# One group of a two-level Strassen-Winograd kernel makes its product S3 x T3 plainly, and the sums of T3's quarters come behind it

## The chip, the core and the metric

The kernel runs on one core of a Trainium2 chip. The time is in device microseconds, from three runs of the same program; the median is given. One further execution was recorded by the profiler, and all times of single instructions come from it. The engines are called PE (TensorE, the matmuls), PEld (its weight loads), DVE (VectorE), ACT (ScalarE), POOL (GpSimd) and SP (SyncE, whose queue issues nearly all DMAs). Each engine works through its own queue in order.

## The reference

```python
def reference(x, w):                       # x: 8 x 2048 x 2048, w: 2048 x 2048, f32
    cs = np.cumsum(x, axis=1)
    diff = cs - np.concatenate([zeros, cs[:, :-1, :]], axis=1)
    return np.matmul(diff, w).astype(np.float32)
```

The difference of a running sum is the input again, so the kernel computes x times w: 16384 rows of x against a 2048 x 2048 matrix.

## The kernel before

The rows of x are cut into 128 row tiles of 128 rows. The first four are multiplied in a head stage while the weights are loaded, and w is scaled and kept on chip as f16 blocks. The rest is done in groups of four row tiles, named g, h (upper half of the two-by-two scheme) and k, l (lower half; k belongs to g, l to h). A group is one step of Winograd's form of Strassen's method: seven products P1 to P7 of half-size blocks, with sums S1 to S4 of x blocks and T1 to T4 of weight blocks. P7 is S3 x T3. The tiles 4 to 7 (`group_plain`) and 8 to 11 (`group_half`) are special; from tile 12 on 29 objects of the class `Group` follow, numbered 0 to 28 here. "The first group of the table" is group 0, tiles 12 to 15.

In a `Group`, P1, P2, P3, P4, P5 and P7 are made once more by seven: each is split into seven quarter products, written P7.p1 to P7.p7, of four 128x512 matmuls each (`quarter`, recorded at L592). Only P6 is made plainly (`whole`), as four pieces for tile g and four for tile h, P6g.0 to P6h.3, of four matmuls each (`steps`, recorded at L573). A product by seven costs 28 matmuls, a plain one 32. By seven it also needs sums on other engines:

- small sums of x quarters, P7.s1 to P7.s4 (128x512 f16, L561 on POOL or L563 on DVE);
- sums of weight quarters. Those that are wanted in every group are kept; the others are made anew in each group, as fills of the one buffer `flow` (P7.fp4, P7.fp5, P7.fp7; 128x2048 f16 on DVE, L958). The kept ones are made once, in or before group 0, by `less` (L555). For T3 they are two, `sums_of_T3` in the code: the first overwrites the quarter t12 of T3 itself with t12 - t11, the second makes t22 minus that. T3 can be used plainly only until the first of them;
- copies of finished quarters from their PSUM bank (ACT, P7.c1, c5, c6, c7 at L1086) and additions of them onto the banks that hold P1 + P6 (DVE, P7.a1, a5g, a5h, a6, a7h, a7k at L1061; P5.m1 and P5.m2 of product P5 have the same line).

The four banks g0, g1, h0, h1 hold P1 + P6 + P7 in the end. From them add.C22g0 to add.C22h1 take an output block (DVE, L603, scaled) and keep.C21... and P4 go on. The additions without a scale, such as add.C12g1.e, are L1127. Banks, buffers c of outputs and four scratch quarters are taken from lists, first freed first used.

What stands in which order is set by a table, `ORDER`: about 260 step names, each with the group it belongs to relative to the running one (P1.p1+1 is the next group's). The loop at the end of the function walks the table once per group and issues each step on its engine. So group 0's P7 is mixed with the end of its P5, with P3, with P4, and with the loading, scaling (weigh, scale, recip, narrow) and transposing (turn) of group 1's tiles. A dictionary `before` hangs the one-time sums of weights ahead of named steps of group 0. S1.g, S3.g, S3.h are the sums S of one tile (128x1024, L563).

Of the kernel before, what the change touches and what calls it, by code (L numbers as in the profile page):

```python
# [10 lines left out]
def kernel(  # L11
# [30 lines left out]
    PLAIN = 4  # L42
    KQ = KO // 4
    END = M // P
# [12 lines left out]
    B11, T1, B12, T2, B21, T3, B22, T4 = (  # L57
        [p[:, i // 2, i % 2] for p in pieces] for i in range(8)
    )
# [4 lines left out]
    def quarter_of(i, a, n):  # L64
        return blocks[:, i // 2, i % 2, ds(4 * a, 4), n, :]

    def spare_of(i, k):
        return blocks[:, i // 2, i % 2, ds(k, 2), :, :]
# [17 lines left out]
    def after(engine, ask):  # L86
        if engine in last:
            with tc.issue_after(last[engine].ins):
                said = ask()
        else:  # L90
            said = ask()
        last[engine] = said[-1] if isinstance(said, tuple) else said
        return said
# [100 lines left out]
    with ExitStack() as head:  # L194
        ring = [alone([P, NH], bf16, f"wb{i}", head) for i in range(7)]
        results = [alone([P, NB], f32, f"o{i}", head) for i in range(5)]
        first = head.enter_context(tc.tile_pool(name="first", bufs=1))
# [276 lines left out]
    class Part:  # L474
        def __init__(self, ap):
            self.all = ap
# [31 lines left out]
    class Inner:  # L508
# [7 lines left out]
        def first(self):  # L516
            less(self.Q1, self.t12, self.t11)
            less(self.Q2, self.t22, self.Q1)
# [19 lines left out]
    def in_twos(t):  # L538
        return t if len(t.shape) == 4 else t.rearrange("p (a b) n -> p a b n", b=2)
# [5 lines left out]
    def half_of(t, i):  # L545
        return in_twos(t)[:, i]
# [5 lines left out]
    def less(dst, p, q):  # L552
        if len(dst.shape) == 4 or len(p.shape) == 4 or len(q.shape) == 4:
            dst, p, q = in_twos(dst), in_twos(p), in_twos(q)
        after("dve", lambda: nc.vector.tensor_tensor(dst, p, q, SUB))  # L555
# [88 lines left out]
    in_5 = Inner(1, spare_of(2, 6), quarter_of(6, 1, 0), flow)  # L644
    in_1 = Inner(0, spare_of(2, 6), S1_all, flow)
# [316 lines left out]
    in_7 = Inner(5, None, quarter_of(5, 0, 1), None)  # L962
# [23 lines left out]
    LATE = 'C12g0 C12g1 C12h1 C12h0 C11g1 C11h1 C21g1 C21h1'.split()  # L986

    class Group:
        def __init__(self, g):
            self.late = LATE if g + 4 < END else ()  # L990
            self.tiles = dict(g=g, h=g + 2, k=g + 1, l=g + 3)
            self.at = {}
            self.do = {}
            self.sums = {}
            self.plan()
# [144 lines left out]
        def plan(self):  # L1140
            tiles = self.tiles
            half = {}
# [13 lines left out]
            def A(c, i):  # L1156
                return [half[c][i].half(n) for n in range(2)]

            x, z = ["h0", "h1", "g0", "g1"], ["zh0", "zh1", "zg0", "zg1"]
# [60 lines left out]
            self.add("C12h1", q, "q")  # L1220
            self.add("C12h0", q, "q", let=True)

            self.small_sums("P7", A("g", 0), A("h", 0), True)
            self.onto("P7", *x)
            for n, c in zip(x, ("C22h0", "C22h1", "C22g0", "C22g1")):
                self.add(c, n, "x")

# [73 lines left out]
    END_ORDER = """  # L1301
# [7 lines left out]
    group_plain(PLAIN, *pairs)  # L1309
    group_half(PLAIN + 4, *pairs[:2], *banks[4:])  # L1310
    open_banks += [banks[i] for i in (6, 7, 0, 1, 3, 5, 2, 4)]
    groups = [Group(g) for g in range(PLAIN + 8, END, 4)]
    for c in groups[0].tiles:
        for s in ("load", "weigh0", "weigh1", "scale", "recip", "unit", "narrow0", "narrow1", "turn0", "turn1"):
            del groups[0].do[f"{s}.{c}"]
# [3 lines left out]
    def first(*names):  # L1319
        return min(names, key=place_of.get)  # L1320

    def sums_of_T3():
        less(in_7.t12, in_7.t12, in_7.t11)
        less(in_7.Q2, in_7.t22, in_7.t12)

    before = {first("P5.s1", "P5.p5"): lambda: less(in_5.Q1, in_5.t22, in_5.Q2), first("P7.fp5", "P7.fp7", "P7.p6", "P7.fp4"): sums_of_T3, first("P1.s4", "P1.fp4", "P1.p6"): lambda: less(*(half_of(t, 0) for t in (in_1.Q2, in_1.t22, in_1.Q1))), first("P5.s3", "P5.p7"): in_5.third}
    for b in range(-early, len(groups) - late):
        for name, ahead in ORDER:
            i = b + ahead
            if 0 <= i < len(groups) and name in groups[i].do:  # L1330
                if i == len(groups) - 1 and name in END_ORDER:
                    continue
                if i == 0 and name in before:
                    before[name]()
                groups[i].do.pop(name)()
    for name in END_ORDER:
        groups[-1].do.pop(name)()
    assert not any(g.do for g in groups)
# [30 lines left out]
```

## Time and profile before

| what | us |
|---|---|
| median of three runs | 1464.87 (1464.37 to 1465.89) |
| the profiled execution, its own time | 1463.69 |
| its span, first to last instruction | 1461.9 |
| PE busy, 6563 matmuls | 1428.8 (98%) |
| DVE busy | 1408.8 (96%) |
| ACT busy | 1160.6 (79%) |
| POOL busy | 356.6 (24%) |

The profiled execution is 1.18 us shorter than the median. Of its time, 1.8 us lie outside the span. The granted clock of TensorE, in parts of the full one, is 0.996 over the whole span. Times of rows are counted from the span's start. In a timeline, instructions of one form that follow each other are one row: start, length, engine, line, operation, output <- inputs, how many, and in brackets the idle time of the engine before it with what ended that.

### The profile page before, as it was taken

The numbers are of one execution on the slowest core, as the hardware profiler recorded it, in microseconds if no ns is written. First come the engines' busy times: TensorE is split into PE (matmuls) and PEld (weight loads), VectorE is DVE, ScalarE is ACT, GpSimd is POOL, SyncE is SP. The second block draws the span as 40 slices with busy tenths as digits, with TensorE's granted clock in tenths as the row PEclk, the third lists the DMA queues.
The fourth block names the chain that finished last, engine by engine and source line by source line (L and its number), as shares of the span: only waits on it lengthen the run. The fifth ranks groups of instructions, "written<-read, shape, count | busy, mean of one in ns | idle before, by whom it ended". The sixth has DMA issues, their size and how long they took to land. (4 is left out here: it accounts for less than half of the span.)

```text
span 1461.9 us, 21138 instructions
## 1 busy us (share of the span) xinstructions
PE 1428.8 (98%) x6563; PEld 635.8 (43%) x6563; DVE 1408.8 (96%) x2367; ACT 1160.6 (79%) x1786; POOL 356.6 (24%) x422
## 2 busy tenths in 40 slices
PE   8999989999999999999999999999999999999997
PEld 3444434444444444444444444444444444444443
DVE  7998899999999999999999999999999999999998
ACT  5887558888788888887888888887888887788882
POOL 0111021223231223321223321222321223221221
PEclk9999999999999999999999999999999999999999
DMA  9999839999898989889998899998889999889992
GB/s 358 368 237 298 213 121 237 240 232 252 228 244 232 250 228 251 236 237 239 238 238 247 238 230 251 251 228 240 241 239 239 252 229 243 229 245 245 248 243 105
DMA packets 377761, 351.65 MB, mean 241 GB/s; under 512 B 274800, under 2 KB 274800, under 8 KB 377520
## 3 DMA queue, kind: packets, MB, share of 16 engines
q1 hardware_dynamic: 377088, 348.47, 88.0%
q0 software_dynamic: 560, 1.84, 0.3%
q8 instruction: 51, 0.84, 0.2%
q14 instruction: 62, 0.51, 0.1%
HBM read 150.99 MB, written 134.22 MB: 195 GB/s over the span
## 5 line engine op out<-in xcount | busy, mean ns | idle before, releaser
L592 PE MATMUL b<-W,x 128*128 128x512 f16 x2124 | 522.3, 380 | 8.2 <-DVE x L563 6.1
L592 PEld LDWEIGHTS <-x 128*128 128x128 f16 x2952 | 286.5, 98 | 372.3 <-DVE x L563 19.6
L1127 DVE TENSOR_TENSOR c<-b,c 128x512 f32<-128x512 f32 x504 | 332.6, 678 | 0.6 <-issue 0.3
L172 ACT ACTIVATE F<-F,of 128x1024 f16<-128x1024 f32 x246 | 283.0, 1150 | 32.6 <-DVE of L156 30.8
L125 ACT ACTIVATE waste<-F 128x1024 uint8<-128x1024 f32 x246 | 259.9, 1057 | 54.5 <-DMA F<-in_x_dram 51.8
L592 PEld LDWEIGHTS <-inner 128*128 128x128 f16 x1996 | 192.6, 98 | 250.3 <-DVE inner L563 27.2
L592 PE MATMUL b<-W,inner 128*128 128x512 f16 x1176 | 288.9, 380 | 1.1 <-DVE inner L563 0.5
L573 PE MATMUL b<-W,x 128*128 128x512 f16 x1216 | 278.0, 379 | 0.3 <-DVE x L563 0.2
L563 DVE TENSOR_TENSOR x<-x,x 128x1024 f16<-128x1024 f16 (+1 forms) x359 | 211.9, 597 | 9.6 <-DMA x<-F 6.3
L603 DVE SCALAR_TENSOR_TENSOR c<-b,of,c 128x512 f32<-128x512 f32 x286 | 209.6, 740 | 8.9 <-PE b L592 5.5
L592 PE MATMUL b<-flow,x 128*128 128x512 f16 x820 | 210.4, 379 | 5.3 <-DVE flow L958 4.3
L600 ACT ACTIVATE c<-b,of 128x512 f32<-128x512 f32 x268 | 178.1, 681 | 37.9 <-PE b L592 13.7
L142 POOL TENSOR_SCALAR of<-of 128x1 f32<-128x1 f32 x112 | 79.5, 710 | 470.1 <-ACT waste L125 412.5
L1061 DVE TENSOR_TENSOR b<-b,c 128x512 f32<-128x512 f32 x290 | 191.6, 687 | 0.2 <-PE b L592 0.2
L1116 ACT COPY c<-b 128x512 f32<-128x512 f32 x224 | 128.5, 579 | 71.4 <-DVE c L603 45.0
L958 DVE TENSOR_TENSOR flow<-W 128x2048 f16<-128x2048 f16 x145 | 184.2, 1270 | 0.0
L573 PEld LDWEIGHTS <-x 128*128 128x128 f16 x1216 | 118.6, 98 | 144.7 <-DVE x L563 7.1
L600 ACT ACTIVATE c<-c,of 128x512 f32<-128x512 f32 x224 | 154.8, 714 | 12.9 <-DVE c L1127 12.9
L592 PE MATMUL b<-inner 128*128 128x512 f16 x472 | 121.1, 379 | 0.0
L561 POOL TENSOR_TENSOR inner<-x 128x512 f16<-128x512 f16 x29 | 35.7, 1232 | 268.2 <-PE b L592 268.2
L561 POOL TENSOR_TENSOR x<-x,x 128x512 f16<-128x512 f16 x58 | 88.3, 1522 | 22.3 <-PE b L592 22.3
L1086 ACT COPY c<-b 128x512 f32<-128x512 f32 x116 | 68.2, 588 | 26.8 <-PE b L592 17.9
(78 smaller groups left out, 988.9 us busy)
## 6 DMA issues: line engine op xcount, KB each, us to landing
F<-in_x_dram SPq DMA_DIRECT2D x246, 512.0 KB, 5.8
out_dram<-c SPq DMA_DIRECT2D x492, 256.0 KB, 3.2
W<-in_w_dram SPq DMA_DIRECT2D x32, 512.0 KB, 9.7
W<-in_x_dram SPq DMA_DIRECT2D x16, 256.0 KB, 7.1
x<-F SPq DMA_TRANSPOSE x246, 3.5
out_dram<-o POOLq DMA_DIRECT2D x5, 256.0 KB, 3.9
out_dram<-o SPq DMA_DIRECT2D x5, 256.0 KB, 3.5
xP<-in_x_dram SPq DMA_DIRECT2D x1, 1024.0 KB, 5.3
```

The costliest lines, as they stand in the source:

```text
L125: lambda: nc.scalar.activation(waste, where[t][i], ABS, scale=1.0 / ROW, accum_out=sums_of[t][:, i : i + 1],),
L172: lambda: nc.scalar.activation(narrowed(t)[:, ds(i * NH, NH)], where[t][i], COPY, scale=s),
L561: after("pool", lambda: nc.gpsimd.tensor_tensor(dst.all, p.all, q.all, op))
L563: after("dve", lambda: nc.vector.tensor_tensor(dst.all, p.all, q.all, op))
L573: said = nc.tensor.matmul(to[n], a[k], b[k][:, n, :], start=(first and k == 0), stop=(k == KH - 1), skip_group_check=True,)
L592: said = nc.tensor.matmul(to, a[k], b[k], start=(first and k == 0), stop=(k == 3), skip_group_check=True)
L600: after("act", lambda: nc.scalar.activation(c, p, COPY, scale=u))
L603: after("dve", lambda: nc.vector.scalar_tensor_tensor(c, p, u, c, MUL, ADD))
L958: after("dve", lambda: nc.vector.tensor_tensor(in_twos(flow), x, y, op))
L1061: after("dve", lambda: nc.vector.tensor_tensor(t, p, s, ADD))
L1116: after("act", lambda: nc.scalar.copy(to, p))
L1127: after("dve", lambda: nc.vector.tensor_tensor(to, p, to, ADD))
```

## The change

In group 0 alone, P7 is made as a whole product like P6. Its sums, fills, copies and additions are not issued there. The pieces of the plain product take the places of some of the quarters in the table: P7g.0 stands where P7.p1 stood, P7g.1 to P7g.3 where P7.p5, P7.p6 and P7.p2 stood, P7h.0 and P7h.1 in the place of P7.a7k, P7h.2 and P7h.3 in that of P7.fp4. The two sums of T3 move from ahead of P7.fp5 to two later places of group 0: one ahead of add.C12g1.e, one ahead of add.C21h1.e. Groups 1 to 28 make P7 by seven, as before.

```diff
     class Group:
-        def __init__(self, g):
+        def __init__(self, g, more):
+            self.more = more
...
-            self.small_sums("P7", A("g", 0), A("h", 0), True)
-            self.onto("P7", *x)
+            if self.more:
+                self.small_sums("P7", A("g", 0), A("h", 0), True)
+                self.onto("P7", *x)
+            else:
+                self.whole("P7", T3, half["g"][0], half["h"][0], *x)
...
-    groups = [Group(g) for g in range(PLAIN + 8, END, 4)]
+    groups = [Group(g, g > PLAIN + 8) for g in range(PLAIN + 8, END, 4)]
...
-    def sums_of_T3():
-        less(in_7.t12, in_7.t12, in_7.t11)
-        less(in_7.Q2, in_7.t22, in_7.t12)
+    PLAINLY = {
+        "P7.p1": ["P7g.0"],
...
+        "P7.a7k": ["P7h.0", "P7h.1"],
+        "P7.fp4": ["P7h.2", "P7h.3"],
+    }
...
-    before = {..., first("P7.fp5", "P7.fp7", "P7.p6", "P7.fp4"): sums_of_T3, ...}
+    before = {..., "add.C12g1.e": lambda: less(in_7.t12, in_7.t12, in_7.t11), "add.C21h1.e": lambda: less(in_7.Q2, in_7.t22, in_7.t12), ...}
+    def go_on(i, name):
+        if i == len(groups) - 1 and name in END_ORDER:
+            return
+        if i == 0 and name in before:
+            before[name]()
+        for some in [name] if groups[i].more else PLAINLY.get(name, [name]):
+            if some in groups[i].do:
+                groups[i].do.pop(some)()
```

The instructions in their order, engine by engine. On DVE, group 0, from the sum that stands ahead of P5.s3 (`W<-W`, then P5.s3) on; before, T3's two sums follow (`x2`), then the fill P7.fp5, S3.h, a reciprocal, and P7.s1, whose result the matmuls of P7.p5 read:

```order
L555 TENSOR_TENSOR W<-W 128x4x512
L563 TENSOR_TENSOR x_69<-x_67,x_69 128x512
L555 TENSOR_TENSOR W<-W 128x4x512 x2
L958 TENSOR_TENSOR flow<-W 128x2048
L563 TENSOR_TENSOR x_65<-x_70,x_65 128x1024
L156 RECIPROCAL of<-of 128x1
L563 TENSOR_TENSOR inner<-x_65 128x512
L563 TENSOR_TENSOR x_66<-x_64,x_66 128x512
L563 TENSOR_TENSOR inner<-inner,x_63 128x512
L1061 TENSOR_TENSOR b_784<-b_784,c_771 128x512
L563 TENSOR_TENSOR x_65<-x_63,x_65 128x512
L563 TENSOR_TENSOR inner<-x_63,inner 128x512
```

After, in the same place:

```order
L555 TENSOR_TENSOR W<-W 128x4x512
L563 TENSOR_TENSOR x_69<-x_67,x_69 128x512
L563 TENSOR_TENSOR x_65<-x_70,x_65 128x1024
L156 RECIPROCAL of<-of 128x1
L563 TENSOR_TENSOR x_66<-x_64,x_66 128x512
L563 TENSOR_TENSOR inner<-inner,x_67 128x512
L603 SCALAR_TENSOR_TENSOR c_751<-b_784,of,c_751 128x512
L603 SCALAR_TENSOR_TENSOR c_759<-b_784,of,c_759 128x512
L563 TENSOR_TENSOR x_67<-x_67,x_68 128x512
L563 TENSOR_TENSOR inner<-inner,x_64 128x512
```

T3's sums, the fill and P7.s1, P7.s2, P7.s3 are gone from here; S3.h, P3.s3 and P5.s2 (`inner<-inner,x_67`) follow directly, and then add.C22g0 and add.C21g0 (L603).

On PE, group 0, behind P6's last piece, one row for each run of four matmuls. Before: P7.p1, P4.p1, P7.p5 (which reads `flow` and a sum), P7.p6, P7.p2 and P5.p5:

```order
L592 MATMUL b_786<-W,x_63 128x512
...
L592 MATMUL b_789<-W,x_68 128x512
...
L592 MATMUL b_790<-flow,inner 128x512
...
L592 MATMUL b_786<-W,inner 128x512
...
L592 MATMUL b_784<-W,x_63 128x512
...
L592 MATMUL b_790<-F,inner 128x512
```

After: P7g.0 (onto two banks in turn), P4.p1, P7g.1 to P7g.3 as one run of twelve, and P5.p5:

```order
L573 MATMUL b_784<-W,x_63 128x512
L573 MATMUL b_787<-W,x_63 128x512
...
L592 MATMUL b_786<-W,x_68 128x512
...
L573 MATMUL b_784<-W,x_63 128x512
L573 MATMUL b_787<-W,x_63 128x512
...
L592 MATMUL b_789<-F,inner 128x512
```

Between P6 and P5.p5 no matmul reads `flow` or a small sum of P7 any more.

On DVE, at the end of group 0, before: the fill P4.fp4, add.C12g1.z, add.C22h0 (L603), add.C12g1.e, add.C21g1, P1.s1 of group 1, a reciprocal, P1.s2, add.C21g1.q, P1.s4, P2.s1, add.C21h1.e:

```order
L958 TENSOR_TENSOR flow<-W 128x2048
L1127 TENSOR_TENSOR c_755<-b_786,c_755 128x512
L603 SCALAR_TENSOR_TENSOR c_747<-b_791,of,c_747 128x512
L1127 TENSOR_TENSOR c_755<-b_790,c_755 128x512
L1127 TENSOR_TENSOR c_763<-b_787,c_763 128x512
L563 TENSOR_TENSOR inner<-x_65 128x512
L156 RECIPROCAL of<-of 128x1
L563 TENSOR_TENSOR inner<-inner,x_63 128x512
L1127 TENSOR_TENSOR c_763<-b_789,c_763 128x512
L563 TENSOR_TENSOR inner<-x_63,inner 128x512
L563 TENSOR_TENSOR inner<-x_66 128x512
L1127 TENSOR_TENSOR c_767<-b_784,c_767 128x512
```

After, from add.C22h0 on:

```order
L603 SCALAR_TENSOR_TENSOR c_751<-b_791,of,c_751 128x512
L555 TENSOR_TENSOR W<-W 128x4x512
L1128 TENSOR_TENSOR c_755<-b_789,c_755 128x512
L1128 TENSOR_TENSOR c_763<-b_787,c_763 128x512
L563 TENSOR_TENSOR inner<-x_65 128x512
L156 RECIPROCAL of<-of 128x1
L563 TENSOR_TENSOR inner<-inner,x_63 128x512
L1128 TENSOR_TENSOR c_763<-b_786,c_763 128x512
L563 TENSOR_TENSOR inner<-x_63,inner 128x512
L563 TENSOR_TENSOR inner<-x_66 128x512
L555 TENSOR_TENSOR W<-W 128x4x512
L1128 TENSOR_TENSOR c_767<-b_790,c_767 128x512
```

The two `W<-W` rows are T3's sums: one stands ahead of add.C12g1.e and so ahead of P1.s1, the other between P2.s1 and add.C21h1.e. Lines from 1061 on have a number higher by one.

More of the change, by code (lines that the diff above doesn't have):

```diff
@@ L1320, in first @@
         return min(names, key=place_of.get)
-    def sums_of_T3():
-        less(in_7.t12, in_7.t12, in_7.t11)
-        less(in_7.Q2, in_7.t22, in_7.t12)
-    before = {first("P5.s1", "P5.p5"): lambda: less(in_5.Q1, in_5.t22, in_5.Q2), first("P7.fp5", "P7.fp7", "P7.p6", "P7.fp4"): sums_of_T3, first("P1.s4", "P1.fp4", "P1.p6"): lambda: less(*(half_of(t, 0) for t in (in_1.Q2, in_1.t22, in_1.Q1))), first("P5.s3", "P5.p7"): in_5.third}
+    PLAINLY = {
+        "P7.p1": ["P7g.0"],
+        "P7.p5": ["P7g.1"],
+        "P7.p6": ["P7g.2"],
+        "P7.p2": ["P7g.3"],
+        "P7.a7k": ["P7h.0", "P7h.1"],
+        "P7.fp4": ["P7h.2", "P7h.3"],
+    }
+    before = {first("P5.s1", "P5.p5"): lambda: less(in_5.Q1, in_5.t22, in_5.Q2), "add.C12g1.e": lambda: less(in_7.t12, in_7.t12, in_7.t11), "add.C21h1.e": lambda: less(in_7.Q2, in_7.t22, in_7.t12), first("P1.s4", "P1.fp4", "P1.p6"): lambda: less(*(half_of(t, 0) for t in (in_1.Q2, in_1.t22, in_1.Q1))), first("P5.s3", "P5.p7"): in_5.third}
+    def go_on(i, name):
[6 more added lines that the diff above has]
+                groups[i].do.pop(some)()
     for b in range(-early, len(groups) - late):
         for name, ahead in ORDER:
[L1329 to L1335, printed above, removed]
+            if 0 <= b + ahead < len(groups):
+                go_on(b + ahead, name)
     for name in END_ORDER:
```

## The prediction

> **What bounds the kernel now.** I read the page's first part, then TensorE's (PE's) timeline around the place of the change, then VectorE's (DVE's) timeline there, then the table by stretches.
>
> ```profile
> PE 1428.8 (98%) x6563; PEld 635.8 (43%) x6563; DVE 1408.8 (96%) x2367; ACT 1160.6 (79%) x1786; POOL 356.6 (24%) x422
> 180.00:225.00 45.00, 39.42 (x167) 16.61 (x165) 41.47 (x62) 24.89 (x41) 10.64 (x12) 0.92 0.43 128
> 199.70:203.00 3.30, 3.28 (x8) 1.19 (x9) 2.92 (x6) 2.40 (x4) 0.00 (x0) 0.50 0.01 2
> 450.00:460.00 10.00, 8.48 (x41) 3.62 (x39) 8.39 (x15) 8.08 (x13) 0.30 (x1) 1.00 1.08 219
> ```
>
> In the stretches the columns are length, busy time (instructions) of PE, weight loads, DVE, ACT and POOL, then granted clock, DMA share and GB/s. PE and DVE are both nearly full over the whole span, so neither can be loaded without a price; but the 45 us that hold the first group of the table have PE at 39.42 and DMA at 0.43 only. PE's timeline of that place follows (start, length, then the idle time before a row and what ended it). By the order of the steps, 189.15 is P6h, 193.53 P7.p1 and P4.p1, then come P7.p5, P7.p6, P7.p2, P5.p5 and P7.p7; 218.33 begins with P3.p4, 223.51 is P4.p4, 224.44 P1.p5 of the next group, 227.91 begins with P1.p3, and 235.50 is P5.p1.
>
> ```profile
> 189.15 3.62 PE L573 MATMUL b<-W,x 128*128 128x512 f16 x16
> 193.53 1.90 PE L592 MATMUL b<-W,x 128*128 128x512 f16 x8 [0.76 <-DVE x L563]
> 199.72 1.89 PE L592 MATMUL b<-flow,inner 128*128 128x512 f16 x4 [4.29 <-DVE inner L563]
> 201.40 1.91 PE L592 MATMUL b<-W,inner 128*128 128x512 f16 x4
> 203.10 1.91 PE L592 MATMUL b<-W,x 128*128 128x512 f16 x4
> 204.81 1.44 PE L592 MATMUL b<-F,inner 128*128 128x512 f16 x4
> 206.09 1.03 PE L592 MATMUL b<-flow,x 128*128 128x512 f16 x4
> ...
> 218.33 1.89 PE L592 MATMUL b<-W,x 128*128 128x512 f16 x8
> ...
> 223.51 1.03 PE L592 MATMUL b<-flow,x 128*128 128x512 f16 x4
> 224.44 1.04 PE L592 MATMUL b<-W,inner 128*128 128x512 f16 x4
> ...
> 227.91 1.91 PE L592 MATMUL b<-W,inner 128*128 128x512 f16 x8
> ...
> 235.50 1.04 PE L592 MATMUL b<-W,x 128*128 128x512 f16 x4 [0.50 <-DVE x L563]
> ```
>
> A row's length runs to its last matmul's end, so rows overlap; a quarter product (four matmuls) takes (3.62 - 1.03) / 3 = 0.863 us from start to start at full clock, by the rows of 16 (189.15) and of 4 (206.09). I use 0.865, since the lengths are rounded. At 199.72 PE has stood 4.29 us, waiting for a DVE sum, and the clock is 0.50 when it resumes: the four quarters from 199.72 to 206.09 take 6.37 us, where 4 x 0.865 = 3.46. So the idle time costs 2.91 us a second time. DVE in the same place: S3.g, a sum for P5, P5.s3, T3's two sums, P7.fp5, P7.s1; then add.C22h1 (219.13), add.C12g1.e and add.C21g1 (222.78), and of the next group P1.s1, a reciprocal, P1.m1 (227.11), a reciprocal and S1.g:
>
> ```profile
> 192.79 0.68 DVE L563 TENSOR_TENSOR x<-x,x 128x1024 f16<-128x1024 f16 x1
> 193.40 1.21 DVE L555 TENSOR_TENSOR W<-W 128x2048 f16<-128x2048 f16 x1
> 194.53 0.41 DVE L563 TENSOR_TENSOR x<-x,x 128x512 f16<-128x512 f16 x1
> 194.86 2.47 DVE L555 TENSOR_TENSOR W<-W 128x2048 f16<-128x2048 f16 x2
> 197.37 1.22 DVE L958 TENSOR_TENSOR flow<-W 128x2048 f16<-128x2048 f16 x1
> ...
> 199.23 0.42 DVE L563 TENSOR_TENSOR inner<-x 128x512 f16<-128x512 f16 x1
> ...
> 219.13 0.73 DVE L603 SCALAR_TENSOR_TENSOR c<-b,of,c 128x512 f32<-128x512 f32 x1
> ...
> 222.78 1.27 DVE L1127 TENSOR_TENSOR c<-b,c 128x512 f32<-128x512 f32 x2
> 223.98 0.41 DVE L563 TENSOR_TENSOR inner<-x 128x512 f16<-128x512 f16 x1
> 224.50 0.16 DVE L156 RECIPROCAL of<-of 128x1 f32<-128x1 f32 x1
> ...
> 227.11 0.69 DVE L1061 TENSOR_TENSOR b<-b,c 128x512 f32<-128x512 f32 x1
> ...
> 234.09 0.16 DVE L156 RECIPROCAL of<-of 128x1 f32<-128x1 f32 x1 [0.45 <-POOL of L142]
> 234.76 1.41 DVE L563 TENSOR_TENSOR x<-x,x 128x1024 f16<-128x1024 f16 x2
> ```
>
> DVE has no gap from 192.79 to 199.65: PE's wait ends when P7.s1 ends (199.23 + 0.42 = 199.65; the matmul starts at 199.72). Ahead of it in DVE's queue stand T3's two sums (194.86, two of 1.21, 197.37 less 194.86 = 2.51 from start to start) and the fill P7.fp5 (197.37). Start to start, one such 128x2048 sum takes 1.13 us (193.40 to 194.53), a 128x512 f16 sum 0.33 (194.53 to 194.86), a 128x1024 one 0.61 (192.79 to 193.40). Each of these is some 0.07 less than the row's length, and I take the same off the others: 0.66 for the 0.73 at 219.13.
>
> **The change, part by part.**
>
> *Removed from DVE in group 0*: three fills (3 x 1.13), four small sums (4 x 0.33), six additions onto banks. *From ACT*: four copies.
>
> ```profile
> L1061 DVE TENSOR_TENSOR b<-b,c 128x512 f32<-128x512 f32 x290 | 191.6, 687 | 0.2 <-PE b L592 0.2
> L1086 ACT COPY c<-b 128x512 f32<-128x512 f32 x116 | 68.2, 588 | 26.8 <-PE b L592 17.9
> ```
>
> Six additions at 0.687 are 4.1 us, together 8.8 us of DVE; four copies at 0.588 are 2.4 us of ACT. ACT's part is worth nothing in itself: it was busy 24.89 of 45 us. DVE's part counts only as far as PE waited for it, up to 218.33.
>
> *Added to PE*: seven quarters become a whole product of 32 matmuls, eight quarters' worth: +0.865 us, all on the path.
>
> *PE's walk, first piece.* Its first plain piece waits for S3 of tile g (192.79), as P7.p1 does now: 193.53 stays. P7g.0, P4.p1, P7g.1 to P7g.3 follow without a wait, since T3 itself was made long before: P5.p5 at 197.85. P4.p2 goes onto a bank that add.C22g0 has to read first; that addition starts when P7g.3 ends (198.06) and takes 0.73, so P4.p2 starts at 198.84 (0.12 lost). P5.p6 at 199.70 has its sum: P5.s2 now follows S3.h, the reciprocal and P3.s3, so it is done by 196.4 (194.86 + 0.61 + 0.16 + 2 x 0.33). P3.p1 at 200.57. P5.p3 waits for P5.m1: DVE does add.C21g0 (199.91, when P4.p2 ends; 0.66), two sums (0.33 each), then P5.m1 from 201.23 to 201.92 (0.69, as at 227.11); P5.p3 starts at 201.96 and not at 201.43, 0.53 lost. Then P5.p7, P3.p6, P4.p6, P5.p4, P3.p7, P3.p3 and the four pieces of P7h run on: P3.p4 starts at 211.48. Before, it starts at 218.33. As a sum: 24.80 us now for 19 quarters (16.43 of work, 8.37 of waits and half clock) against 20 quarters (17.30) and 0.65 of new waits: 17.95. Gain here 6.85.
>
> *What now waits.* add.C22h1 (219.13 now) needs P7h, which ends at 211.64; DVE reaches it near 209.2, behind three additions for P3.p7 and P5 (207.4 + 3 x 0.6), and stands 2.5 us. Behind it in DVE's queue are add.C12h0 up to P1.s1 of the next group, so the 8.8 us taken off DVE don't become a lead. It starts at 211.68, 7.45 earlier than now.
>
> *T3's two sums, 1.13 each, in their new places.* The first stands between add.C22h0 and add.C12g1. From add.C22h1 to P1.s1 DVE takes 4.85 now (219.13 to 223.98); then 4.85 + 0.21 (add.C12h0 waits for P3.p4) + 1.13 = 6.19, so P1.s1 starts at 217.87 and P1.p5 at 218.33, where PE alone would be there at 217.53. Against 224.44 the gain is 6.11. The second stands before add.C21h1. From P1.s1 to P1.m1: 3.13 now, plus 1.13, less the 0.19 that DVE stood before 224.50 (0.52 between starts, 0.33 of work): P1.m1 at 221.94, P1.p3 at 222.67 (the now 227.91). Gain 5.24. From P1.m1 to S1.g: 7.65 now, of it 0.45 of waiting for POOL at 234.09, which goes because DVE comes later than POOL's result; S1.g at 229.14, P5.p1 0.74 behind it at 229.88. Against 235.50 the gain is 5.62. From there both engines run in the same order, shifted alike.
>
> *Bounds of the sums' price.* Hidden altogether, and with PE's 0.50 before 235.50 gone: gain 6.85 + 0.50 = 7.35. Paid in full: 6.85 - 2.26 = 4.59. I take 5.62, from the walk.
>
> *The queues that the change moves past.*
>
> ```profile
> 205.09 1.24 SPq L185 DMA_TRANSPOSE x<-F  x1
> 218.57 2.62 SPq L185 DMA_TRANSPOSE x<-F  x2
> ```
>
> SP's transposes of the next group wait for the last reader of their tile: the first for P7's last use of tile g (203.10, ending 205.01), the pair for P7's last use of tile h. Both move forward with PE: P7g.3 ends at 198.0, P7h.3 at 211.6. The loads behind them use a DMA that is 0.43 busy here. POOL's sums only wait for DVE and PE, and its queue is idle in 34 of these 45 us. So the inputs of group 1 move forward by some 6 us too.
>
> *The clock.* No idle time of the walk is over 0.9 us, so I take the 2.91 as gained whole; at 456.10 (below) PE stood 1.52 us in a stretch whose clock is 1.00.
> [...]
>
> **The sum.** The profiled execution took 1463.69 us, 1.18 under the median of the runs. 1463.69 - 5.62 = 1458.07; for the median 1464.87 - 5.62 = 1459.25. What is left open is how later groups fall:
>
> ```profile
> 313.39 1.03 PE L592 MATMUL b<-S,inner 128*128 128x512 f16 x4
> 356.71 1.03 PE L592 MATMUL b<-S,inner 128*128 128x512 f16 x4
> 401.60 1.03 PE L592 MATMUL b<-S,inner 128*128 128x512 f16 x4
> 456.10 1.04 PE L592 MATMUL b<-W,x 128*128 128x512 f16 x4 [1.52 <-DVE x L563]
> 1410.12 1.03 PE L592 MATMUL b<-S,inner 128*128 128x512 f16 x4
> ```
>
> The rows of b<-S,inner are one product (P1.p6) in different groups. A group takes 43.32 us, or 44.89 where DVE waited for input and PE for DVE; the 25 groups from 313.39 to 1410.12 average 43.87. One such wait more or fewer is 1.5 us either way.
>
> **The rivals.**
> *The half clock comes back.* The new waits at 201.4, 217.5 and 221.8 (0.53, 0.80, 0.88) fall within 21 us. Were they to bring the half clock once, at 2.91, the gain would be 2.71: 1462.2. Against it: 450 to 460 with 1.52 us of idle time in one piece kept 1.00.
> [...]
> *The input chain holds its pace* and group 1 waits for its tiles: gain 0, 1464.9. Against it: DMA 0.43, and the transposes wait for PE's reads.
> *Slower: every later group takes the long form.* PE and DVE now meet the input with another phase; if all 25 groups took 44.89, that would be 25 x 1.02 = 25.5 us, 1484.7. It ends slower from 0.23 us per group (5.62 / 25). Against it: the order from group 1 on is unchanged, banks are only renamed, and inputs gain as much as PE.
> *The sums stay hidden*: 1457.5.
>
> **How the numbers follow.** The walk, with the sums priced between hidden and paid in full, 0.78; hidden altogether 0.06. Half clock 0.06, input chain 0.05 (gain under 2.9), slower 0.05. A measurement here tells 0.2% (2.9 us) from no change; the three runs lie within 1.5 us. So faster 0.84, same 0.11, slower 0.05. The range goes from 1457.5 less 1.3 to the half-clock case: 1456.2 to 1462.2.
>
> **What would show it.** Right: no idle of PE above 1 us between 193 and 236; clock 1.00 in 195 to 206; P3.p4 near 211.5; DVE standing about 2.5 us before add.C22h1; a 0.8 us wait for P1.s1; the group after starting 5.6 earlier. Wrong: PE waiting at a plain piece; P1.m1 later than 223; a new wait of ACT for input behind 205; or later groups averaging other than 43.87.

## The result and the profile after

| kernel | runs | median us | lowest to highest | ratio to before, 95% |
|---|---|---|---|---|
| before | 7 | 1464.87 | 1462.38 to 1467.59 | |
| after | 7 | 1460.02 | 1458.56 to 1461.91 | 0.997 (0.9958 to 0.9981) |

The change gains 4.85 us (1464.87 - 1460.02), 0.3%; 1459.25 was predicted for the median. The profiled execution of after took 1461.91 us, 1.89 above its median, where that of before was 1.18 below its own. The two spans (1461.9 and 1459.8) therefore show only 2.1 us of the gain, and the traces are compared place by place.

Of after, first the page's busy times, then the table by stretches, with the columns described in the prediction:

```profile
PE 1428.9 (98%) x6567; PEld 634.9 (43%) x6567; DVE 1398.8 (96%) x2354; ACT 1159.6 (79%) x1782; POOL 356.7 (24%) x422
```

```profile
180.00:225.00 45.00, 41.99 (x193) 18.46 (x191) 36.58 (x58) 27.97 (x44) 10.33 (x12) 1.00 0.61 167
195.00:206.00 11.00, 10.19 (x48) 4.58 (x47) 7.69 (x15) 8.17 (x13) 6.05 (x6) 1.00 0.84 215
```

In the 45 us of group 0, PE is busy 41.99 us instead of 39.42, and the granted clock is 1.00 instead of 0.92. DVE's busy time over the whole span fell by 10.0 us (8.8 predicted; 8.4 between the second traces of both kernels, 1409.1 and 1400.7). PE's timeline of the place follows (the lines behind the diff have numbers one higher in after: L1062 and L1128 are the former L1061 and L1127):

```profile
193.50 1.04 PE L573 MATMUL b<-W,x 128*128 128x512 f16 x4 [0.76 <-DVE x L563]
...
195.23 2.75 PE L573 MATMUL b<-W,x 128*128 128x512 f16 x12
...
198.69 1.03 PE L592 MATMUL b<-W,x 128*128 128x512 f16 x4
...
202.25 1.02 PE L592 MATMUL b<-W,inner 128*128 128x512 f16 x4 [0.81 <-DVE b L1062]
...
208.29 3.62 PE L573 MATMUL b<-W,x 128*128 128x512 f16 x16
211.75 1.89 PE L592 MATMUL b<-W,x 128*128 128x512 f16 x8
...
218.61 1.04 PE L592 MATMUL b<-W,inner 128*128 128x512 f16 x4 [0.66 <-DVE inner L563]
219.49 1.03 PE L592 MATMUL b<-S,inner 128*128 128x512 f16 x4
...
223.01 1.96 PE L592 MATMUL b<-W,inner 128*128 128x512 f16 x8 [0.78 <-DVE b L1062]
...
230.12 1.04 PE L592 MATMUL b<-W,x 128*128 128x512 f16 x4
```

At 195.23, where P7.p5 stood for 4.29 us before, the twelve matmuls of P7g.1 to P7g.3 start behind P4.p1 without a wait. P7h (208.29) runs on into P3.p4 (211.75). Three waits of 0.81, 0.66 and 0.78 us are left. DVE's timeline shows what they wait for: add.C22g0 and add.C21g0, P5.m1, add.C22h1, the first sum of T3, P1.s1, the second sum, P1.m1, a reciprocal and S1.g:

```profile
197.81 0.75 DVE L603 SCALAR_TENSOR_TENSOR c<-b,of,c 128x512 f32<-128x512 f32 x1 [1.57 <-PE b L573]
200.17 0.75 DVE L603 SCALAR_TENSOR_TENSOR c<-b,of,c 128x512 f32<-128x512 f32 x1 [1.61 <-PE b L592]
...
201.51 0.69 DVE L1062 TENSOR_TENSOR b<-b,c 128x512 f32<-128x512 f32 x1
...
211.95 0.75 DVE L603 SCALAR_TENSOR_TENSOR c<-b,of,c 128x512 f32<-128x512 f32 x1 [2.43 <-PE b L573]
...
215.81 1.22 DVE L555 TENSOR_TENSOR W<-W 128x2048 f16<-128x2048 f16 x1
...
218.14 0.41 DVE L563 TENSOR_TENSOR inner<-x 128x512 f16<-128x512 f16 x1
...
220.20 1.22 DVE L555 TENSOR_TENSOR W<-W 128x2048 f16<-128x2048 f16 x1
...
222.27 0.69 DVE L1062 TENSOR_TENSOR b<-b,c 128x512 f32<-128x512 f32 x1
...
228.72 0.16 DVE L156 RECIPROCAL of<-of 128x1 f32<-128x1 f32 x1
...
229.38 1.41 DVE L563 TENSOR_TENSOR x<-x,x 128x1024 f16<-128x1024 f16 x2
```

DVE now stands for PE, where before PE stood for DVE: 2.43 us before add.C22h1, for P7h. The 0.45 us wait for POOL at the last reciprocal is gone. SP's queue, the two transposes that the prediction names:

```profile
198.06 1.25 SPq L185 DMA_TRANSPOSE x<-F  x1
...
211.99 2.62 SPq L185 DMA_TRANSPOSE x<-F  x2
```

They stood at 205.09 and 218.57 before, so the inputs of group 1 came 7.0 and 6.6 us earlier.

### The profile page after: what moved, and what is told of

It reads as the page before. It is cut to its first block, busy times and chain, and to the rows that moved or that the text cites. A ratio compares the mean times of both kernels' runs of the same rounds, so it can differ in the third digit from the quotient of the medians.

```text
span 1459.8 us, 21125 instructions
## 1 busy us (share of the span) xinstructions
PE 1428.9 (98%) x6567; PEld 634.9 (43%) x6567; DVE 1398.8 (96%) x2354; ACT 1159.6 (79%) x1782; POOL 356.7 (24%) x422
## 5 line engine op out<-in xcount | busy, mean ns | idle before, releaser
L1128 DVE TENSOR_TENSOR c<-b,c 128x512 f32<-128x512 f32 x504 | 333.5, 680 | 1.8 <-PE b L592 1.7
L603 DVE SCALAR_TENSOR_TENSOR c<-b,of,c 128x512 f32<-128x512 f32 x286 | 210.3, 743 | 12.8 <-PE b L592 5.8
L1062 DVE TENSOR_TENSOR b<-b,c 128x512 f32<-128x512 f32 x284 | 188.4, 691 | 1.9 <-ACT c L1087 1.0
L958 DVE TENSOR_TENSOR flow<-W 128x2048 f16<-128x2048 f16 x142 | 179.0, 1260 | 0.0
L561 POOL TENSOR_TENSOR inner<-x 128x512 f16<-128x512 f16 x29 | 35.8, 1234 | 269.0 <-PE b L592 259.1
L561 POOL TENSOR_TENSOR x<-x,x 128x512 f16<-128x512 f16 x58 | 89.7, 1547 | 21.4 <-PE b L592 21.4
```

The costliest lines, as they stand in the source:

```text
L561: after("pool", lambda: nc.gpsimd.tensor_tensor(dst.all, p.all, q.all, op))
L603: after("dve", lambda: nc.vector.scalar_tensor_tensor(c, p, u, c, MUL, ADD))
L958: after("dve", lambda: nc.vector.tensor_tensor(in_twos(flow), x, y, op))
L1062: after("dve", lambda: nc.vector.tensor_tensor(t, p, s, ADD))
L1128: after("dve", lambda: nc.vector.tensor_tensor(to, p, to, ADD))
```

## The experiments

Three questions were left. Is the idle time what brings the half clock? What do T3's two sums cost in their new places? And does what group 0 gains reach the end, 28 groups later? For the last, a marker is used: the start of P1.p6 in group 1, which is the row of b<-S,inner at 219.49 above and the same row in each other trace. What comes after it is the median time less the marker. The marker is of the one execution that was traced, the median of all; where the traced execution is not like the median one, the difference mixes the two, and this matters for two rows below. The kernel before ran beside every set, with medians of 1464.2 to 1464.8.

The table holds all kernels in the order of the marker; the sections below tell what each is.

| kernel | marker | median us (runs) | ratio to before, 95% | median less marker |
|---|---|---|---|---|
| e8_two_fills | 225.77 | 1464.89 (12) | 1.0 (0.9989 to 1.0011) | 1239.12 |
| before | 225.32 | 1464.87 (7) | | 1239.55 |
| b2_before | 224.96 | 1464.82 (11) | 1.0003 (0.9991 to 1.0014) | 1239.86 |
| e5_filler8 | 224.04 | 1465.02 (10) | 0.9997 (0.9983 to 1.0012) | 1240.98 |
| e6_after_fill16 | 222.74 | 1462.02 (12) | 0.9987 (0.9974 to 0.9999) | 1239.28 |
| e11_fill16_16 | 222.14 | 1461.49 (12) | 0.9977 (0.9966 to 0.9987) | 1239.35 |
| e9_fill32 | 222.00 | 1462.34 (12) | 0.9992 (0.9980 to 1.0004) | 1240.34 |
| e1_filler16 | 221.95 | 1465.86 (12) | 0.9994 (0.9982 to 1.0006) | 1243.91 |
| e7_short16 | 221.85 | 1466.39 (11) | 1.0007 (0.9995 to 1.0019) | 1244.54 |
| e10_seven_no_sums | 220.02 | 1459.58 (12) | 0.9969 (0.9958 to 0.9981) | 1239.56 |
| e4_early_h | 219.66 | 1458.44 (5) | 0.9956 (0.9941 to 0.9971) | 1238.78 |
| a2_after | 219.56 | 1459.39 (12) | 0.9964 (0.9949 to 0.9978) | 1239.83 |
| after | 219.49 | 1460.02 (7) | 0.997 (0.9958 to 0.9981) | 1240.53 |
| e2_no_sums | 218.35 | 1457.39 (6) | 0.9948 (0.9932 to 0.9963) | 1239.04 |

### Sixteen matmuls in the idle time of before

The kernel before, with 16 matmuls ahead of P7.p5 whose result is overwritten. They fill PE's wait and take nothing from DVE's queue.

```diff
+                if i == 0 and name == "P7.p5":
+                    for _ in range(4):
+                        quarter(open_banks[0], groups[0].sums["P4"]["p1"], in_4.weights()["p1"], True)
```

> The kernel before, with 16 matmuls of no use added on TensorE right ahead of P7.p5 of group 0, into the bank that P7.p5 then starts afresh. They fill some 3.5 us of the 4.29 us wait and move nothing else. Theory (the wait costs twice, once as idle time and once as half clock behind it): the clock stays 1.00 from 195 to 206, P7.p5 still starts near 199.7, the four quarters behind it take 3.5 us instead of 6.4. VectorE stood 1.28 + 0.41 + 0.38 us in that stretch, so it becomes the next limit and the gain is 2.0 to 2.9 us against before: about 1462.3. Rival (the slow quarters have another cause than the idle time): same clock row as before, gain 0. [...]

PE's timeline, and the stretch of 11 us in the table by stretches:

```profile
193.26 5.35 PE L592 MATMUL b<-W,x 128*128 128x512 f16 x24 [0.76 <-DVE x L563]
199.45 1.04 PE L592 MATMUL b<-flow,inner 128*128 128x512 f16 x4 [0.83 <-DVE inner L563]
...
202.91 1.03 PE L592 MATMUL b<-flow,x 128*128 128x512 f16 x4
```

```profile
195.00:206.00 11.00, 10.17 (x48) 4.49 (x47) 10.93 (x19) 5.44 (x9) 2.27 (x2) 1.00 0.48 120
```

The idle time shrinks from 4.29 to 0.83 us and the clock is 1.00. The four quarters from 199.45 to 202.91 take 3.46 us, where before took 6.37. So the 2.91 us belong to the idle time, as the prediction had it, and the marker moves 3.37 us forward (225.32 to 221.95). But the median did not: 1465.86 us.

### The change without T3's sums

After, with the two sums left out, and so with wrong weights in P7 of the later groups.

```diff
-    before = {..., "add.C12g1.e": lambda: less(in_7.t12, in_7.t12, in_7.t11), "add.C21h1.e": lambda: less(in_7.Q2, in_7.t22, in_7.t12), ...}
+    before = {...}
```

> The changed kernel without T3's two sums: they are left out altogether, so that the later groups use T3's quarters as they are; it measures their price. Theory: the 0.66 us wait before P1.p5 and the 0.78 us wait before P1.p3 go, P5.p1 of group 1 starts near 229.0 instead of 230.1, and the time is 1.0 to 1.5 us under that of the changed kernel. Rival (the sums cost their full 2.3 us): P5.p1 near 227.9. Rival (the sums are hidden): P5.p1 at 230.1, the same time.

PE's timeline at P1.p5, P1.p3 and P5.p1:

```profile
217.48 1.03 PE L592 MATMUL b<-W,inner 128*128 128x512 f16 x4
...
220.94 1.89 PE L592 MATMUL b<-W,inner 128*128 128x512 f16 x8
...
228.06 1.04 PE L592 MATMUL b<-W,x 128*128 128x512 f16 x4
```

The rows show no wait at any of the three, where in after the first two waited 0.66 and 0.78. This execution started P7g.0 at 193.19, 0.31 earlier than after's; with that taken off, they stand 0.82, 1.76 and 1.75 us earlier than in after. The price of the sums is thus 1.75 of their 2.26 us. The prediction had 7.35 - 5.62 = 1.73 in its bounds. The price expected of this run itself, about 1.1 us at P5.p1, was too low. The median, 1457.39, lies 2.0 us under that of the changed kernel in the same set (1459.39); their intervals overlap.

### The sums and P7h earlier

After, with P7h moved forward and the sums placed where DVE stands waiting.

```diff
-        "P7.a7k": ["P7h.0", "P7h.1"],
-        "P7.fp4": ["P7h.2", "P7h.3"],
+        "keep.C12h1": ["keep.C12h1", "keep.C12h0"],
+        "P7.p7": ["P7h.0", "P7h.1"],
+        "P7.p3": ["P7h.2", "P7h.3"],
...
-    before = {..., "add.C12g1.e": lambda: less(in_7.t12, ...), "add.C21h1.e": lambda: less(in_7.Q2, ...), ...}
+    before = {..., "P5.m2": lambda: less(in_7.t12, ...), "add.C12h1.q": lambda: less(in_7.Q2, ...), ...}
```

> The changed kernel with the four pieces P7h moved forward (two to the place of P7.p7, two to that of P7.p3, with keep.C12h0 issued right behind keep.C12h1), and T3's two sums moved to where VectorE then stands idle: the first ahead of P5.m2, the second ahead of add.C12h1.q. Theory: the waits before P5.p3 (0.81), P1.p5 (0.66) and P1.p3 (0.78) shrink to 0.5 us together, P1.p3 starts near 221 instead of 223.0; at S1.g the reciprocal waits for input again, so 1 to 1.5 us remain at P5.p1. Rival (the price of the sums is a matter of VectorE's total work, not of place): P5.p1 stays at 230.1.

ACT's, DVE's and PE's timelines, one row of each:

```profile
225.76 1.06 ACT L125 ACTIVATE waste<-F 128x1024 uint8<-128x1024 f32 x1 [1.20 <-DMA F<-in_x_dram]
```

```profile
228.85 0.16 DVE L156 RECIPROCAL of<-of 128x1 f32<-128x1 f32 x1 [0.75 <-POOL of L142]
```

```profile
230.30 1.04 PE L592 MATMUL b<-W,x 128*128 128x512 f16 x4 [0.96 <-DVE x L563]
```

P1.p3 starts at 222.25, 0.76 earlier than in after, and not near 221: waits of 0.62 and 0.44 us are left of the first two, and two of 0.28 and 0.54 are new. P5.p1 starts at 230.30, no earlier than after's 230.12. That is the number of the rival, but the rows give another reason: ACT waits for a loaded tile of x, the reciprocal behind it waits 0.75 for POOL, and PE 0.96 for S1.g. So in this kernel the input chain binds at this place. SP issues the loads at 219.23 here, behind outputs, where it is 218.84 in after and 217.87 in the run without the sums, in which the same reciprocal waits only 0.18 and PE not at all. The median is 1458.44, 6.3 us under before. That is not told apart from after: the intervals overlap.

### The change again

> The changed kernel once more, for a second trace of the groups behind group 1. Theory (the later groups scatter by when VectorE waits for input, whatever the change): the times from P1.p6 of group 1 to P1.p6 of group 28, 1184.8 us before and 1188.5 us in the changed kernel's first trace, come out anywhere between these or beyond; no wait stands in a fixed group. Rival (the change costs the later groups some 3.7 us): 1188 to 1189 again, with group 2 again near 45.4 us.

The same kernel in another set of runs: 1459.39 us against 1464.78, a gain of 5.39. The marker stands at 219.56, within 0.07 us of the first trace. From there to P1.p6 of group 28 it takes 1188.0 us, where the first trace of after has 1188.5 and that of before 1184.8. By itself that would bear out the rival, but group 2 has 43.5 and not 45.4, and the second trace of before (below) has 1187.3: this much lies between executions of one kernel.

### How much idle time brings the half clock

The kernel before with 8 matmuls of 512 columns in the idle time, and with 16 of 128 columns (the lines of the first experiment, with `range(2)`, and this):

```diff
+                if i == 0 and name == "P7.p5":
+                    to, a, w4 = open_banks[0], groups[0].sums["P4"]["p1"], in_4.weights()["p1"]
+                    for k in range(16):
+                        after("pe", lambda: nc.tensor.matmul(to[:, :128], a[k % 4], w4[k % 4][:, :128], start=True, stop=True, skip_group_check=True))
```

> The kernel before with 8 matmuls of no use (512 columns) ahead of P7.p5: the idle time before P7.p5 shrinks to some 2.6 us. If 1.5 us (full clock behind it, in the kernel before) and 4.3 us (half clock) bracket the point from which the clock falls, this tells on which side 2.6 us lies: full clock means P7.p6 0.87 us behind P7.p5, half clock 1.7 us.

> The kernel before with 16 matmuls of no use right ahead of P7.p5, as in the kernel with the filled wait, but of 128 columns instead of 512, so that they take about 0.9 us and most of the wait stays open (some 3.4 us). It has the same number of TensorE instructions ahead of every later group as the filled one. Theory A (the filled kernel lost its 3.4 us again in groups 2 to 27 because of when its work fell): here the time from P1.p6 of group 1 to that of group 28 is that of before, 1184 to 1187. Theory B (it lost them because its instructions stand elsewhere in the program): 1190 here too, and a time of 1467 to 1469. Besides it shows whether 3.4 us of idle time bring the half clock.

PE's timeline with the 8 matmuls:

```profile
199.66 1.04 PE L592 MATMUL b<-flow,inner 128*128 128x512 f16 x4 [2.56 <-DVE inner L563]
200.54 1.73 PE L592 MATMUL b<-W,inner 128*128 128x512 f16 x4
202.06 1.91 PE L592 MATMUL b<-W,x 128*128 128x512 f16 x4
203.77 1.21 PE L592 MATMUL b<-F,inner 128*128 128x512 f16 x4
204.81 1.03 PE L592 MATMUL b<-flow,x 128*128 128x512 f16 x4
```

PE's timeline with the 16 short ones:

```profile
194.91 1.06 PE L1339 MATMUL b<-W,x 128*128 128x128 f16 x16
199.35 1.04 PE L592 MATMUL b<-flow,inner 128*128 128x512 f16 x4 [3.39 <-DVE inner L563]
...
202.82 1.03 PE L592 MATMUL b<-flow,x 128*128 128x512 f16 x4
```

An idle time of 2.56 us did bring the half clock, and it came only after PE had resumed: the first quarter (199.66) took the usual 0.88 to the next start, the second 1.52 and the third 1.71. From 199.66 to 204.81 are 5.15 us, 1.69 lost. An idle time of 3.39 us brought none: 199.35 to 202.82 are 3.47. Its length alone does not decide.

What goes with the half clock shows in the granted clock, read in narrow stretches. In these traces it changes only at points that lie 3.413 us apart, or a multiple of that; the stretch from one point to the next is called a window here. The clock is 0.50 from 198.81 to 205.64 in before and from 200.71 to 204.12 with the 8 matmuls, which is 6.83 and 3.41 us, two windows and one. Its last fall, at the kernel's end, comes 367 and 369 windows behind (1458.33 and 1463.64). Counted back from the last fall of the kernel with the short matmuls (1460.61), windows begin there at 194.27 and 197.68, so its idle time, 195.97 to 199.35, is split between two. The table by stretches, one row for each window, of before, with the 8 matmuls, and with the 16 short ones:

```profile
195.40:198.81 3.41, 0.03 (x1) 0.00 (x0) 3.34 (x4) 0.00 (x0) 0.00 (x0) 1.00 0.89 247
198.81:202.23 3.42, 2.51 (x6) 0.89 (x7) 3.04 (x9) 2.21 (x4) 0.00 (x0) 0.50 0.12 49
202.23:205.64 3.41, 3.41 (x9) 1.21 (x8) 1.98 (x3) 2.22 (x3) 1.15 (x1) 0.50 0.00 0
```

```profile
197.30:200.71 3.41, 1.05 (x5) 0.50 (x6) 3.39 (x7) 1.46 (x2) 0.00 (x0) 1.00 0.52 205
200.71:204.12 3.41, 3.41 (x9) 1.22 (x8) 2.41 (x6) 2.88 (x5) 1.02 (x1) 0.50 0.00 0
```

```profile
194.27:197.68 3.41, 1.69 (x20) 1.16 (x18) 3.34 (x4) 0.56 (x1) 0.00 (x0) 1.00 0.94 225
197.68:201.10 3.42, 1.75 (x9) 0.80 (x10) 3.42 (x9) 2.15 (x4) 0.00 (x0) 1.00 0.34 137
```

A window in which PE was busy for 0.03 or 1.05 us of 3.41 was followed by the half clock; the windows with 1.69 and 1.75 were not. In all fourteen traces, from 30 us on, every window with 1.05 us or less is followed by half clock (three of them here and in the second trace of before, the others at the kernel's end), and no window at full clock with 1.64 or more is (the 1.64 is of e10_seven_no_sums, below, around its wait of 1.77 us: 3.41 - 1.77). Where the limit lies between these two is not shown. Once the clock was at half, the window with 2.51 us did not end that, and the one that was busy throughout did. What is lost is half of the time at half clock in which PE has work: (205.64 - 199.72) / 2 = 2.96 for the 2.91 of before, and 3.41 / 2 = 1.71 for the 1.69 here.

The windows begin at other times in each trace (198.81, 198.16 and 200.71 are the falls of three), so the same wait can fall into one window or be split between two. And a window need not be idle throughout to bring the half clock, as the 1.05 us of work show.

### Before, once more

> The kernel before once more, for a second trace: group 0 the same to 0.1 us (4.3 us wait, half clock of 5 to 6 us, P1.p6 of group 1 near 225.3); from there to P1.p6 of group 28 1184.8 us in the first trace, which was 1.2 us under the median, so 1184 to 1189 here.

1464.82 us (ratio 1.0003). The half clock returned in the same form: PE resumed at 199.65, and the four quarters took 6.08 us (to 205.73). That is 2.62 us lost and not 2.91; the clock was 0.50 from 198.16 to 204.99, behind a window with 0.61 us of work.

Not every execution loses the same. Each comes with its mean clock, and one window at half clock takes an estimated 3.41 / 2 / 1462 = 0.0012 off it: the traces with two such windows in group 0 have 0.996 and 0.997, that with one 0.998, those with none 0.999. Of the 104 executions of before that ran beside the sets, 50 have 0.995 to 0.997, 47 have 0.998 and 7 have 0.999; all 19 of after have 0.999 or 1.000. The medians of the 104 follow the clock: 1466.30 us at 0.996 (13), 1465.28 at 0.997 (36), 1464.11 at 0.998 (47) and 1462.97 at 0.999 (7). So the half clock's cost reaches the end, as far as these medians show, and the trace that the prediction read (0.996) is of the dearer half.

### Where the filled kernels lose their gain

The first experiment left something open: 3.4 us earlier at the marker, nothing at the end. Either a group 0 by seven gives back what it gained, or the added matmuls cost something later. Against each other stood: after with the 16 matmuls ahead of P7g.1; before without T3's two sums (they are left out, and no matmul is added); before with 16 matmuls more, ahead of P3.p5; with 32 of 256 columns in place of 16 of 512; with 16 of 512 and 16 of 64. The edits in this order:

```diff
+            if i == 0 and some == "P7g.1":
+                for _ in range(4):
+                    quarter(open_banks[0], groups[0].sums["P4"]["p1"], in_4.weights()["p1"], True)
```

```diff
     def sums_of_T3():
-        less(in_7.t12, in_7.t12, in_7.t11)
-        less(in_7.Q2, in_7.t22, in_7.t12)
+        pass
```

```diff
+                if i == 0 and name in ("P7.p5", "P3.p5"):
+                    for _ in range(4):
+                        quarter(open_banks[0], groups[0].sums["P4"]["p1"], in_4.weights()["p1"], True)
```

```diff
+                    for k in range(32):
+                        after("pe", lambda: nc.tensor.matmul(to[:, :256], a[k % 4], w4[k % 4][:, :256], start=True, stop=True, skip_group_check=True))
```

```diff
+                    for _ in range(4):
+                        quarter(open_banks[0], groups[0].sums["P4"]["p1"], in_4.weights()["p1"], True)
+                    for k in range(16):
+                        after("pe", lambda: nc.tensor.matmul(to[:, :64], a[k % 4], w4[k % 4][:, :64], start=True, stop=True, skip_group_check=True))
```

> The changed kernel with 16 matmuls of no use (512 columns) right ahead of P7g.1 in group 0: TensorE is 3.46 us later from there on, and everything that waits for it. If what group 0 gains or loses stays to the end, the time is that of the changed kernel plus 3.0 to 3.5 us, about 1463. If the later groups give back what group 0 gains, as they did behind the filled wait, it is that of the changed kernel or at most 1 us more.

> The kernel before (P7 by seven in group 0) without T3's two sums: they are left out, so the later use of T3's quarters is not the reference's. TensorE's instructions are the same as before, none added. P7.p5 comes 2.3 us earlier, after a wait of 2.0 us; if the clock stays full behind it, P1.p6 of group 1 comes at 220.5 to 222 instead of 225.2. Theory A (with P7 by seven, what group 0 gains by an earlier P7.p5 is lost again in the later groups): the time is that of before within 1.5 us, 1464 to 1466, and P1.p6 of group 1 to that of group 28 takes 1188 to 1191. Theory B (it was the added TensorE instructions that cost the later groups): the gain stays, 1459.5 to 1461.5, and the later groups take 1184 to 1187.

> The kernel with the filled wait (16 matmuls of no use ahead of P7.p5) and 16 more ahead of P3.p5 of group 0, which take 3.5 us of TensorE's time, so that P1.p6 of group 1 is back at 224.5 to 225.5. Theory A (the later groups give and take by when group 0 ends): about the time of before, 1464 to 1466, later groups 1184 to 1187. Theory B (added TensorE instructions cost the later groups some 4 us): 1468 to 1470.

> The kernel before with 32 matmuls of no use of 256 columns ahead of P7.p5: the same 3.5 us of filling as with 16 of 512, so group 0 is the same as there (P1.p6 of group 1 near 222), with 32 instructions more on TensorE instead of 16. Theory A (time alone decides): 1465 to 1467 as with 16, later groups 1189 to 1191. Theory B (the place of instructions decides): another time, anywhere from 1461 to 1467.

> The kernel before with the 16 matmuls of no use of 512 columns ahead of P7.p5, as in the first filled kernel, and 16 more of 64 columns behind them, which fill another 0.5 to 0.9 us of the same wait: group 0 is the same (P1.p6 of group 1 near 222), the number of added TensorE instructions is that of the kernel with 32 of 256 columns. If the number of instructions is what cost the later groups their 4 us with 16 and not with 32, the time is that with 32: 1461.5 to 1463. If it is the size or the time of the filling, it is that with 16: 1465 to 1467.

PE's timeline of before without T3's sums, at P7.p5 and at the marker:

```profile
197.53 1.04 PE L592 MATMUL b<-flow,inner 128*128 128x512 f16 x4 [1.77 <-DVE inner L563]
...
220.02 1.03 PE L592 MATMUL b<-S,inner 128*128 128x512 f16 x4
```

P7.p5 waits 1.77 us there, the clock stays full, and the marker moves 5.30 forward. The median, 1459.58, moves 4.64 against the 1464.22 beside it. So group 0 by seven keeps its gain, and the first idea falls. This run also shows where the change's gain comes from: with P7 still by seven, the two sums taken from ahead of P7.s1 give nearly as much as the whole change. The plain product is what lets them stand later.

As a rule the second idea falls too. Sixteen matmuls more (1464.89), 16 + 16 (1461.49) and the 16 in after (1462.02) all end where their marker says. So does 32 (1462.34), though its interval still takes in no change. Twelve of the table's fourteen rows have 1238.8 to 1241.0 us behind the marker. Only the two versions of before with 16 added matmuls and no more have some 4 us more.

For the 16 short ones that is in part the clock. Their traced execution (0.999) had no half clock, but 8 of their 11 executions have 0.997 or 0.998, so the median is of another kind than the marker. The three with 0.999 have a median of 1464.82, 1243.0 behind the marker: some 3 us too many, on three executions. With 8 matmuls it is the other way round: the traced execution had the half clock, and seven of ten have 0.999 or 1.000, so that row shows little. The first experiment is free of this (all 12 at 0.999 or 1.000), and its 4 us stand. One total is higher in the traces of these two versions than in the others, the wait of DVE's row sums for transposed tiles. First that group by lines for the first experiment, then for after (busy, mean ns, idle time before and what ended it):

```profile
L563 DVE TENSOR_TENSOR x<-x,x 128x1024 f16<-128x1024 f16 (+1 forms) x359 | 212.2, 598 | 13.1 <-DMA x<-F 9.8
```

```profile
L563 DVE TENSOR_TENSOR x<-x,x 128x1024 f16<-128x1024 f16 (+1 forms) x358 | 211.7, 598 | 10.2 <-DMA x<-F 6.7 <-issue 0.3
```

9.8 us against 6.7, and 9.6 in the kernel with 16 short matmuls; all others have 5.5 to 7.6. But the traced execution with 8 matmuls took as long behind its marker, by the spans (1467.0 - 224.04 = 1243.0 us, against 1464.0 - 221.95 = 1242.0 in the first experiment), with a total of 7.4. So this total does not settle where the 4 us go, and the cause stays open.

## Why the prediction was right

*What bound the kernel.* Right in each part. The 4.29 us were the wait for P7.s1 behind T3's sums and the fill, and the 2.91 us came from that idle time (first experiment). No idle time of PE above 1 us is left between 193 and 236, and the clock is 1.00 from 195 to 206.

*PE's and DVE's walk.* Every step came within 0.4 us:

| step | predicted | after |
|---|---|---|
| P4.p2, its wait | 0.12 | none |
| P5.p3, its wait | 201.96, 0.53 | 202.25, 0.81 |
| P3.p4 | 211.48 | 211.75 |
| add.C22h1, DVE's wait | 211.68, 2.5 | 211.95, 2.43 |
| P1.s1 | 217.87 | 218.14 |
| P1.p5, its wait | 218.33, 0.80 | 218.61, 0.66 |
| P1.m1 | 221.94 | 222.27 |
| P1.p3, its wait | 222.67, 0.88 | 223.01, 0.78 |
| S1.g | 229.14 | 229.38 |
| P5.p1 | 229.88 | 230.12 |

The gain at P5.p1 is 235.50 - 230.12 = 5.38 us; 5.62 was predicted. The difference is there from one step on, P5.p3. Before P5.m1 DVE makes add.C21g0, which was put at 199.91 and started at 200.17. Its bank's last matmuls belong to P4.p2, whose row ends at 199.72; why DVE starts 0.45 us behind that, the rows do not show. P4.p2 itself did not wait the 0.12: add.C22g0 started at 197.81, before the modelled end of P7g.3 (195.23 + 2.75 = 197.98).

*The sums' price.* 1.73 by the walk, 1.75 by the run without them. They stand behind DVE's wait of 2.43 us and not in it, and behind it only 0.51 us of them (2.26 - 1.75) find PE with time to spare.

*The input chain.* The transposes came 7.0 and 6.6 us earlier, as expected of a queue that waits for PE's reads: they start at 198.06 and 211.99, each 0.08 us behind the modelled end of P7g.3 (197.98) and of P7h (208.29 + 3.62 = 211.91). The rival in which it holds its pace fell here. That it can bind, a little further on, shows in the kernel with the sums moved earlier still.

*The half clock* did not come back with three waits of 0.66 to 0.81 us in 21 us: PE was busy for at least 2.60 of 3.41 us in each window of after from 194.20 to 224.92. The clock over 180 to 225 is 1.00. Between the two traces the marker moved 5.83 us (225.32 to 219.49) and P5.p1 5.38, of which the 2.91 of the half clock is a part.
The 2.91 is the size of one execution, though. Two windows at half clock gave it; the second trace has 2.62, and by their clocks an estimated half of the executions of before have one window or none. With the 1.69 us that one window took from the kernel with the 8 matmuls in place of the 2.91, the walk would give an estimated gain of 5.62 - 2.91 + 1.69 = 4.40. The medians cannot tell that from 5.62 (by its ratio, the first gain lies between 2.8 and 6.2 us), so it is partly luck that 1460.02 came within 0.77 us of the forecast.

*Later groups.* The prediction let the 28 groups run as before, give or take 1.5 us, and named another average than 43.87 us for 25 of them as a sign that it is wrong. The traces of after have 43.95 and 44.01, but the second trace of before has 43.96: 43.87 was the number of one execution, and between executions the later groups differ by more than 1.5 us. So the sign says nothing either way, and the medians have to. The table's last column supports the prediction: 1239.55 and 1239.86 us for before, 1240.53 and 1239.83 for after. The medians' gains, 4.85 and 5.39, lie below and at the 5.38 of the trace. The rival in which every later group takes the long form would have needed 25 us there.

## What to carry to other kernels

A one-time sum that stands in the queue of a full engine is best placed where that engine will stand anyway, and an operand that is still whole lets its first user run without the sum; the run without the sums shows how much of the price is left. Here an idle time of TensorE cost more than its length where it left one of these windows with little work, 1.05 of 3.41 us or less (4.29 us cost 2.91 more, 2.56 us 1.69 more), so measure the quarters after it too, and look at the mean clock of every execution and not only of the traced one. Compare two versions at a marker just behind the edit and by the medians: in this pipeline of 28 groups one profiled execution was up to 3.7 us off its median (1468.76 against 1465.02 with the 8 matmuls).

## What was not expected

*The clock can fall after the work has resumed.* With 2.56 us of idle time the half clock began 1.05 us behind the resumption (199.66; 200.71), at the end of a window, while 3.39 us, split between two windows, brought none. In before it fell at 198.81, 0.91 ahead of the resumption.

*Where a DVE fill and a POOL sum start together, one of the two takes some 1 us longer.* In after, DVE's and POOL's timelines (two places each) and PE's:

```profile
254.61 1.22 DVE L958 TENSOR_TENSOR flow<-W 128x2048 f16<-128x2048 f16 x1
...
299.28 2.10 DVE L958 TENSOR_TENSOR flow<-W 128x2048 f16<-128x2048 f16 x1
```

```profile
254.61 2.24 POOL L561 TENSOR_TENSOR x<-x,x 128x512 f16<-128x512 f16 x1 [0.62 <-PE b L592]
...
299.15 1.16 POOL L561 TENSOR_TENSOR x<-x,x 128x512 f16<-128x512 f16 x1 [0.49 <-PE b L592]
```

```profile
301.43 1.02 PE L592 MATMUL b<-flow,x 128*128 128x512 f16 x4 [0.65 <-DVE flow L958]
```

A fill takes 1.22 us at 254.61, and the POOL sum that starts in the same moment takes 2.24 instead of 1.16. At 299.28 POOL was there 0.13 us before; the fill takes 2.10, and PE waits 0.65 for it. The fill that started in the same moment kept its own length, and so did the POOL sum that started 0.13 us before. There are 3 to 9 fills of over 2 us behind group 0 in each trace (7 in before, 6 in after, 3 in the kernel with P7h earlier), and PE's waits for fills come to 4.1, 3.7 and 1.5 us there, so this is a part of the scatter between executions.
In after 27 single POOL sums (L561) start within 0.14 us of a single fill, and in each of these pairs one takes longer. The 21 long POOL sums (2.19 to 2.29 us) start at most 0.06 us before or behind a fill of 1.21 to 1.23; the six long fills (2.10 to 2.14) start 0.10 to 0.14 behind a POOL sum of 1.15 or 1.16. The longer one takes a little under the 1.22 + 1.16 = 2.38 us of both.
